# A two-layer encoder step on one core: weight subtractions moved from GpSimd to VectorE in one stage, a sum of squares and bias tiles rearranged in another

## The chip, the core and the metric

The kernel runs on one NeuronCore of a Trainium2 chip. TensorE (PE in the profile) multiplies matrices, VectorE (DVE), ScalarE (ACT) and GpSimd (POOL) work element by element, and SyncE (SP) issues most of the transfers. Each engine takes its own list of instructions strictly in order and waits on semaphores for the others. The metric is device microseconds for one execution: a median of 976.74 us over three runs (975.36 to 978.28).

## The reference

The input is 256 prompt frames and 32 sample frames of width 1024, 288 columns in all, and 256 memory tokens. There are two layers, each with a mixer, a cross-attention into the memory and an MLP. The mixer of layer 0 projects to q, k and v and runs two kinds of softmax attention side by side, 8 heads each: A (a band with a bias by relative position) and B (with a decay made of summed log gates). The mixer of layer 1 is C, stick-breaking attention with 16 heads. Cut to what the change touches:

```python
# memory, both layers: RMS norm over the 1024 features, then k and v
k, v = jnp.split(rmsnorm(mem, g_mem) @ w_kv, 2, axis=-1)
k = rmsnorm(k.reshape(b, n, N_HEADS_X, HEAD_DIM_X), k_gain)

# B: s + decay, masked, softmax;  decay = c_q - c_k
s = jnp.where(ok, s + decay.astype(jnp.float32), NEG)
p = jax.nn.softmax(s, axis=-1)

# C: weights from log_sigmoid(-z), summed from the right
log_keep = jnp.where(before, jax.nn.log_sigmoid(-z), 0.0)
tail = lax.cumsum(log_keep, axis=3, reverse=True) - log_keep
w = jnp.where(before, jnp.exp(jax.nn.log_sigmoid(z) + tail), 0.0)
```

## The kernel before, in words

**Split products.** Activations lie with features on the partitions and the 288 columns along the free axis. Each fp32 operand is split into a high part (`h`, rounded to the PE's reduced fp32 format) and a low part (`l`, the rest), and a product is the three matmuls high·high, high·low, low·high (`mm3`, lines 158 to 160). A weight chunk is 1024 x 256 numbers. `load_chunk` (L118) loads it in two halves into `raw`, one of four buffers shared with the memory's features (`mraw`). ScalarE, or for every n-th piece VectorE (L141), rounds a piece of two rows of blocks into `wh` (L143), and VectorE, or for every n-th piece GpSimd, subtracts it from `raw` into `wl` (L144). The table `STEP` gives each stage the piece's size, which piece's subtraction goes to GpSimd, and which piece's rounding goes to VectorE. A chunk takes 48 matmuls into two PSUM banks out of three (`ps_g`). The next chunk starts in the free bank and needs a bank of the last chunk after three matmuls, so an eviction that is late stops PE there.

**Stages.** A and B with the memory's keys of layer 0, then cross-attention and MLP of layer 0, then C with the memory's keys of layer 1, then cross-attention and MLP of layer 1. Outside C a scheduler orders the instructions of every engine when the kernel is built, by its own estimate of times. In C the order on PE is written out by hand.

**A and B** (`ORD_AB`). Steps `q`, `p` and `a` project q and k, project v, and attend, for one group of four heads. `group_ab` (L923) loads a group's bias tiles: `b1` and `bsmp`, and for B `b0`, on which GpSimd adds the query's sum (L937) and sets the causal mask (L938). There is one buffer of each, so a group's tiles are loaded when the group before has read its own. Step `M` (`mem_split`, L300) splits the memory into `mh` and `ml` and sums its squares, on GpSimd, into `mssum`. The products with `ones` (`ps_ms`, L322 and L325) and the inverse roots `memrs` and `memrt` follow in the same step. `K0` to `K3` are the memory's key projections: their products need only `mh` and `ml`, their eviction `tmk` (L357) needs `memrs`.

**C** (`ORD_C`, `Mix`, L552). `Mix` yields the products of the steps `q`, `k`, `v` (projections for groups 0 to 3), `M` (split of the memory) and `m` (its keys) in pieces of 6 or 12 matmuls. `attend_c` (L641) takes them as filling: it asks for q and k of its group, fills 12 matmuls, computes scores `zz` (prompt, two tiles) and `zs` (sample), starts the softplus chain on ScalarE and VectorE, fills 96 matmuls (`FILL_C[0]`), sums with triangular matmuls (L716, L717), fills 30, multiplies by v for the prompt (L484, result read by `oh` and `ol`, L498 and L499) and at once for the sample (L494), whose result lies in the second half of the tile that `ol` reads. The norm of a key `m` (`xnorm`: `sqx`, `sh`, `sl`, two matmuls `ps_xn`) is put on PE 36 matmuls after the products of that key.

Of the kernel before, what the change touches and what calls it, by code (L numbers as in the profile page):

```python
# [14 lines left out]
P = 128  # L15
# [13 lines left out]
HPE = 0  # L29
HPG = 0  # L30
VT2 = 1
ORD_AB = 'qA0 pA0 F qA1 pA1 aA0 qB0 aA1 qB1 M pB0 pB1 aB0 K2 aB1 K0 K3 K1'.split()
ORD_C = 'q0 k0 v0 q1 M k1 v1 q2 m0 k2 v2 q3 k3 v3 m1 m2 m3'.split()
FILL_C = 96, 30
ORD_X = 's1 s2 s3 s0 v0 v1 S v2 v3'.split()
NWARM = 9
SQP = (0, 1, 2, 3)
# [4 lines left out]
VTB = 2  # L42
WR = 4
WS = 12
STEP = {'ab': (2, 4, 0), 'x0': (4, 5, 7), 'm0': (1, 5, 6), 'c': (2, 2, 4), 'x1': (2, 2, 3), 'm1': (2, 5, 0)}
EPS = 1e-6
NEG = -1e30
EOFF = 160
# [3 lines left out]
def body(ctx: ExitStack, tc: tile.TileContext, i: dict, o: dict):  # L52
# [43 lines left out]
    def bank(pool, name):  # L96
        return pool.tile([P, 512], F32, tag="b", name=name)
# [20 lines left out]
    def load_chunk(ap, w=CW, split=2, before=None):  # L118

        nk = KT // split  # L120
        ws = []
        for s in range(split):
            raw = wraw.tile([P, nk, w], F32, tag="raw", name="raw")
            if before is None:
                nc.sync.dma_start(out=raw, in_=ap[:, s * nk:(s + 1) * nk, :])
            nq = min(nk, NQ) if split > 1 else nk
            step = min(nq, R.step) if before is None else 1
            for k in range(0, nk, step):
                if k % nq == 0:
                    wh = wspl.tile([P, nq, w], F32R, tag="wh", name="wh")  # L130
                    wl = wspl.tile([P, nq, w], F32R, tag="wl", name="wl")
                    ws += [(wh[:, j, :], wl[:, j, :]) for j in range(nq)]
                r, src = slice(k % nq, k % nq + step), raw[:, k:k + step, :]
                if before is not None:
                    nc.sync.dma_start(out=src, in_=ap[:, s * nk + k:s * nk + k + 1, :])
                    before(s * nk + k)
                R.count += 1
                e = nc.gpsimd if R.count % R.pool_every == 0 and before is None else dve
                with ahead(HPS):
                    if R.dve_every and R.count % R.dve_every == 0 and before is None:  # L140
                        dve.tensor_copy(wh[:, r, :], src)  # L141
                    else:
                        act(wh[:, r, :], src, AF.Copy)  # L143
                    e.tensor_tensor(wl[:, r, :], src, wh[:, r, :].bitcast(F32), ALU.subtract)  # L144
        return ws
# [154 lines left out]
    def mem_split(layer):  # L300
        mh = spp.tile([P, KT, T], F32R, tag="sp", name="mh")
        ml = spp.tile([P, KT, T], F32R, tag="sp", name="ml")
        if layer == 0:
            ssum = scr.tile([P, T], F32, tag="ssum", name="mssum", bufs=2)
        for k in range(KT):
            if k % 4 == 0:
                raw = wraw.tile([P, 4, NP_], F32, tag="raw", name="mraw")
                nc.sync.dma_start(out=raw, in_=i["memT"][:, k:k + 4, :])
            m = raw[:, k % 4, :]
            g = gT[:, 3, layer, k:k + 1]  # L310
            act(mh[:, k, 0:NP_], m, AF.Copy, scale=g)
            dve.scalar_tensor_tensor(ml[:, k, 0:NP_], m, g, mh[:, k, 0:NP_].bitcast(F32), ALU.mult, ALU.subtract)
            if layer == 0:
                if k == 0:
                    nc.gpsimd.tensor_tensor(ssum[:, 0:NP_], m, m, ALU.mult)
                else:
                    sq = scr.tile([P, T], F32, tag="f", bufs=FB, name="sqm")
                    nc.gpsimd.tensor_tensor(sq[:, 0:NP_], m, m, ALU.mult)
                    nc.gpsimd.tensor_tensor(ssum[:, 0:NP_], ssum[:, 0:NP_], sq[:, 0:NP_], ALU.add)
        if layer == 0:  # L320
            ps = bank(R.m, "ps_ms")
            mm(ps[:, 0:NP_], ones, ssum[:, 0:NP_], start=True, stop=True)  # L322
            rstd_of(ps[:, 0:NP_], NP_, 1.0 / 1024, memrs)
            for j in range(2):
                mm(ps[:, NP_ + j:NP_ + j + 1], ssum[:, j * P:(j + 1) * P], ones[:, 0:1], start=True, stop=True)  # L325
            rstd_of(ps[:, NP_:NP_ + 2], 2, 1.0 / 1024, memrt)
        return mh, ml

    def sum_parts(ps, sel, sq, n):

# [221 lines left out]
    class Mix:  # L552
# [44 lines left out]
        def run(self, steps):  # L597
            xh, xl, rs = self.x
            for step in steps:
                op, g = step[0], int(step[1:] or 0)  # L600
                if op == "M":
                    mem = mem_split(1)
                elif op == "q":
                    qz = R.ph.tile([P, 2, T], F32, tag="qz", name="qz", bufs=QZB[1])
                    yield from self.products(i["sb_w"][g], xh, xl)
                    for p in range(2):
                        dve.scalar_tensor_tensor(qz[:, p, :], self.ps[p][:, 0:T], 0.125, rs, ALU.mult, ALU.mult)  # L607
                    self.done["q", g] = qz
                elif op == "k":
                    kT = R.ph.tile([P, 2, T], F32, tag="kT", name="kT", bufs=KTB[1])  # L610
                    yield from self.products(i["sb_w"][4 + g], xh, xl)
                    for p in range(2):
                        dve.tensor_tensor(kT[:, p, :], self.ps[p][:, 0:T], rs, ALU.mult)
                    nc.gpsimd.dma_start(out=o["ckT"][:, 2 * g:2 * g + 2, :], in_=kT)
                    self.done["k", g] = kT
                elif op == "v":
                    vT = scr.tile([P, 2, T], F32, tag="t2", name="vT")
                    vt = R.ph.tile([P, 3, CW], F32, tag="vt", name="vt", bufs=VTB)

                    nc.gpsimd.memset(vt[:, 2, :], 0.0)  # L620
                    yield from self.products(i["sb_w"][8 + g], xh, xl)
                    for p in range(2):
                        dve.tensor_tensor(vT[:, p, :], self.ps[p][:, 0:T], rs, ALU.mult)
                    nc.gpsimd.dma_start(out=o["cvT"][:, 2 * g:2 * g + 2, :], in_=vT)

                    def turn(p, vT=vT, vt=vt, g=g):
                        turn_v(vT, vt, p)
                        if p:
                            self.done["v", g] = vt

                    self.later(18, lambda turn=turn: turn(0))
                    self.later(36, lambda turn=turn: turn(1))
                else:
                    yield from self.products(i["w_kv"][1, g], *mem, NP_)
                    t = scr.tile([P, 2, T], F32, tag="t2", name="tmk")
                    for d in range(2):
                        dve.tensor_tensor(t[:, d, 0:NP_], self.ps[d][:, 0:NP_], memrs, ALU.mult)
                    self.later(36, lambda t=t, g=g: self.done.update({("m", g): mem_k_norm(1, g, t)}))
            self.mem = mem

    def attend_c(g, qz, kT, vt, ck, cv, oh, ol, fill):  # L641
# [87 lines left out]
        for p, (zz, w) in enumerate(zip(zzs, wps)):  # L729
            pv_prompt(zz[:, 0, :], p, vt, [(block(w, e, 0), block(w, e, 1)) for e in range(2)])  # L730
            put_prompt(oh, ol, kt0 + p, zz[:, 0, :])
        po = zzs[1][:, 1, :]
        pv_sample(po, cv, vt, [pt[:, 0:P], pt[:, P:2 * P], pt[:, 2 * P:384]], lambda p, par: (2 * p + par) * NS)
        put_sample(oh, ol, kt0, po)
# [186 lines left out]
        return project_v("ab_w", 6 * kind + 4 + g, xh, xl, rs, "ab"[kind] + "vT", g)  # L921

    def group_ab(kind, g, qz, kT, vt):  # L923
        b1 = R.ph.tile([P, 4, NP_], F32, tag="b1", name="b1")
        bsmp = R.ph.tile([P, T], F32, tag="bsmp", name="bsmp")
        if kind == 0:
            nc.sync.dma_start(out=b1, in_=i["biasp"][:, 4 * g:4 * g + 4, :])
            nc.gpsimd.memset(b1[0:64, :, 192:256], NEG)
# [1 line left out]
            nc.sync.dma_start(out=bsmp, in_=i["biass"][g])  # L930
        else:
            nc.sync.dma_start(out=b1, in_=cd[4 * g:4 * g + 4, 0:NP_].unsqueeze(0).to_broadcast([P, 4, NP_]))
            b0 = R.ph.tile([P, 4, P], F32, tag="b0", name="b0")
            for j, d in ((0, b0), (1, b1)):
                n = (j + 1) * P
                cqj = cq[:, j, 4 * g:4 * g + 4].unsqueeze(2).to_broadcast([P, 4, n])
# [15 lines left out]
    for step in ORD_AB:  # L952
        op, at = step[0], step[1:]
        kind, g = ("AB".index(at[0]), int(at[1])) if len(at) == 2 else (0, 0)
        if op == "q":
            qk[at] = project_ab(kind, g)
        elif op == "p":
            vs[at] = values_ab(kind, g)
        elif op == "a":
            group_ab(kind, g, *qk[at], vs[at])  # L960
        elif op == "F":
            forget()
        elif op == "M":
            mh, ml = mem_split(0)
        else:
            R.after = last_mm[0].ins if at == "0" else R.after
            mk0[int(at)] = mem_k(0, int(at), mh, ml)
# [141 lines left out]
```

## Time and profile before

| what | value |
|---|---|
| median of three runs | 976.74 us (975.36 to 978.28) |
| the profiled execution's own time | 978.44 us |
| its span, first to last instruction | 976.1 us |
| PE busy | 952.5 us (98%) |
| DVE busy | 691.8 us (71%) |
| ACT busy | 524.8 us (54%) |
| POOL busy | 266.8 us (27%) |
| mean granted TensorE clock | 0.990 |

The profiled execution took 978.44 us, of which 2.3 us lie outside the span. The page lists busy time for each engine and cuts the span into slices, with the granted TensorE clock beside them. A table of waits says which engine stood idle, at which line, and which instruction of another engine ended the wait. The timeline lists instructions with start and duration, both in microseconds.

### The profile page before, as it was taken

To read this page: it belongs to the slowest core of one execution; us is meant where nothing else is said; L and a number is where in the kernel's file an instruction comes from. 1 tells how busy PE (TensorE), PEld (TensorE's weight loads), DVE (VectorE), ACT (ScalarE), POOL (GpSimd) and SP (SyncE) were. 2 spreads that over 40 slices of the span, in tenths; PEclk is the share of its full clock that TensorE was granted. 3 is DMA by queue.
4 is the path that set the end of the run, shared out by engine and by line. 5 is a ranking of instruction groups with operands and counts; after the bars stand their busy time and mean duration, and the time that the engine had idled before them with its cause. 6 is when DMAs were issued, how large, how long until landed. Compare 5 with 4: busy or idle time off the path is not lost. (4 is left out here: it accounts for less than half of the span.)

```text
span 976.1 us, 19332 instructions
## 1 busy us (share of the span) xinstructions
PE 952.5 (98%) x7284; PEld 920.4 (94%) x7284; DVE 691.8 (71%) x1439; ACT 524.8 (54%) x1212; POOL 266.8 (27%) x275
## 2 busy tenths in 40 slices
PE   8999998999999999999999989899999999999998
PEld 8898787999999999999998889899999999999998
DVE  8778857879777766777677566678987766564643
ACT  5667556656446644444447546555544555453531
POOL 4221363311112211121134233344443211111210
PEclk8999998999999999999999999999999999999999
DMA  8554363654455555545546444365444455455552
GB/s 261 185 174 159 103 223 96 219 184 158 153 168 170 173 162 162 172 155 171 167 159 200 141 143 142 116 231 186 146 148 134 158 171 164 163 164 172 163 171 73
DMA packets 50700, 160.01 MB, mean 164 GB/s; under 512 B 6296, under 2 KB 12968, under 8 KB 50352
## 3 DMA queue, kind: packets, MB, share of 16 engines
q1 hardware_dynamic: 46864, 148.69, 47.6%
q0 software_dynamic: 2592, 8.92, 2.3%
q10 hardware_dynamic: 1152, 1.18, 0.4%
q8 instruction: 57, 0.93, 0.4%
q14 instruction: 35, 0.29, 0.1%
HBM read 148.65 MB, written 10.12 MB: 163 GB/s over the span
## 5 line engine op out<-in xcount | busy, mean ns | idle before, releaser
L143 ACT ACTIVATE wh<-raw 128x512 fp32r<-128x512 f32 (+3 forms) x541 | 269.2, 547 | 234.0 <-PE g L159 107.6
L144 DVE TENSOR_TENSOR wl<-raw,wh 128x512 fp32r<-128x512 f32 (+3 forms) x459 | 309.6, 707 | 99.4 <-ACT wh L143 94.5
L144 POOL TENSOR_TENSOR wl<-raw,wh 128x512 fp32r<-128x512 f32 (+2 forms) x165 | 209.1, 1268 | 532.8 <-ACT wh L143 410.6
L158 PE MATMUL g<-xh,wh 128*128 128x288 f32 (+1 forms) x1032 | 305.0, 299 | 2.9 <-DVE qz L607 1.8
L159 PE MATMUL g<-xl,wh 128*128 128x288 f32 (+1 forms) x1032 | 304.3, 297 | 1.8 <-DVE xl L196 1.8
L160 PE MATMUL g<-xh,wl 128*128 128x288 f32 (+1 forms) x1032 | 303.2, 297 | 0.1
L158 PEld LDWEIGHTS g<-xh,wh 128*128 128x128 f32 (+1 forms) x1032 | 192.9, 188 | 5.0 <-DVE qz L607 2.6
L159 PEld LDWEIGHTS g<-xl,wh 128*128 128x128 f32 (+1 forms) x1032 | 193.5, 188 | 2.7 <-DVE xl L196 2.2
L160 PEld LDWEIGHTS g<-xh,wl 128*128 128x128 f32 (+1 forms) x1032 | 193.1, 188 | 2.6 <-DVE wl L144 1.3
L159 PE MATMUL g<-hl,wh 128*128 128x288 f32 x512 | 150.3, 295 | 0.0
L158 PE MATMUL g<-hh,wh 128*128 128x288 f32 x512 | 149.0, 295 | 0.0
L160 PE MATMUL g<-hh,wl 128*128 128x288 f32 x512 | 148.7, 294 | 0.0
L159 PEld LDWEIGHTS g<-hl,wh 128*128 128x128 f32 x512 | 96.1, 188 | 0.0
L160 PEld LDWEIGHTS g<-hh,wl 128*128 128x128 f32 x512 | 95.8, 188 | 0.0
L158 PEld LDWEIGHTS g<-hh,wh 128*128 128x128 f32 x512 | 95.3, 187 | 0.0
L159 PE MATMUL g<-ol,wh 128*128 128x288 f32 x256 | 75.1, 295 | 0.0
L160 PE MATMUL g<-oh,wl 128*128 128x288 f32 x256 | 74.6, 295 | 0.0
L158 PE MATMUL g<-oh,wh 128*128 128x288 f32 x256 | 74.1, 295 | 0.0
L141 DVE CAST wh<-raw 128x256 fp32r<-128x256 f32 (+2 forms) x83 | 31.9, 384 | 46.3 <-PE g L159 24.5
L867 DVE TENSOR_TENSOR h<-h,g 128x288 f32<-128x288 f32 x64 | 28.8, 450 | 29.7 <-PE g L160 29.6
L159 PEld LDWEIGHTS g<-ol,wh 128*128 128x128 f32 x256 | 48.0, 188 | 0.0
L160 PEld LDWEIGHTS g<-oh,wl 128*128 128x128 f32 x256 | 48.0, 188 | 0.0
(285 smaller groups left out, 1500.0 us busy)
## 6 DMA issues: line engine op xcount, KB each, us to landing
raw<-in_w_up_dram SPq DMA_DIRECT2D x64, 512.0 KB, 3.8
raw<-in_w_down_dram SPq DMA_DIRECT2D x64, 512.0 KB, 3.8
raw<-in_w_kv_dram SPq DMA_DIRECT2D x32, 512.0 KB, 3.9
raw<-in_sb_w_dram SPq DMA_DIRECT2D x24, 512.0 KB, 3.8
raw<-in_ab_w_dram SPq DMA_DIRECT2D x22, 512.0 KB, 5.0
raw<-in_w_q_dram SPq DMA_DIRECT2D x16, 512.0 KB, 4.4
raw<-in_w_o_dram SPq DMA_DIRECT2D x16, 512.0 KB, 4.0
raw<-in_ab_wo_dram SPq DMA_DIRECT2D x8, 512.0 KB, 4.8
```

What stands on the lines that cost most here:

```text
L141: dve.tensor_copy(wh[:, r, :], src)
L143: act(wh[:, r, :], src, AF.Copy)
L144: e.tensor_tensor(wl[:, r, :], src, wh[:, r, :].bitcast(F32), ALU.subtract)
L158: mm(out, lh, rh, start=first, stop=False)
L159: mm(out, lh, rl, start=False, stop=False)
L160: return mm(out, ll, rh, start=False, stop=last)
L867: dve.tensor_tensor(h[:, kt, :], h[:, kt, :], ps[:, 0:T], ALU.add)
```

## The change

In C, `pool_every` becomes 0: all subtractions of weights are VectorE's. A third filling of 12 matmuls stands between the prompt's and the sample's product with v. The order of steps changes: the memory is split after group 1's projections instead of before them, and the keys `m0` and `m1` stand elsewhere. In A and B, `b1`, `bsmp` and `b0` get two buffers each. The memory's squares are ScalarE's and their sums VectorE's. The products with `ones` become a step `N` of their own (`mem_rms`) behind `aB0`, held behind the last projection issued by then.

```diff
-ORD_AB = 'qA0 pA0 F qA1 pA1 aA0 qB0 aA1 qB1 M pB0 pB1 aB0 K2 aB1 K0 K3 K1'.split()
-ORD_C = 'q0 k0 v0 q1 M k1 v1 q2 m0 k2 v2 q3 k3 v3 m1 m2 m3'.split()
-FILL_C = 96, 30
+ORD_AB = 'qA0 pA0 F qA1 pA1 aA0 qB0 aA1 qB1 M pB0 pB1 aB0 N K2 aB1 K0 K3 K1'.split()
+ORD_C = 'q0 k0 v0 q1 k1 v1 M q2 k2 m0 v2 q3 k3 m1 v3 m2 m3'.split()
+FILL_C = 96, 30, 12
-STEP = {..., 'c': (2, 2, 4), ...}
+STEP = {..., 'c': (2, 0, 4), ...}
-                e = nc.gpsimd if R.count % R.pool_every == 0 and before is None else dve
+                e = nc.gpsimd if R.pool_every and R.count % R.pool_every == 0 and before is None else dve
...
-                    nc.gpsimd.tensor_tensor(ssum[:, 0:NP_], m, m, ALU.mult)
+                    act(ssum[:, 0:NP_], m, AF.Square)
...
-                    nc.gpsimd.tensor_tensor(sq[:, 0:NP_], m, m, ALU.mult)
-                    nc.gpsimd.tensor_tensor(ssum[:, 0:NP_], ssum[:, 0:NP_], sq[:, 0:NP_], ALU.add)
-        if layer == 0:
-            ps = bank(R.m, "ps_ms")
...
-        return mh, ml
+                    act(sq[:, 0:NP_], m, AF.Square)
+                    dve.tensor_tensor(ssum[:, 0:NP_], ssum[:, 0:NP_], sq[:, 0:NP_], ALU.add)
+        return mh, ml, ssum if layer == 0 else None
+
+    def mem_rms(ssum):
+        ps = bank(R.m, "ps_ms")
+        mm(ps[:, 0:NP_], ones, ssum[:, 0:NP_], start=True, stop=True)
+        rstd_of(ps[:, 0:NP_], NP_, 1.0 / 1024, memrs)
+        for j in range(2):
+            mm(ps[:, NP_ + j:NP_ + j + 1], ssum[:, j * P:(j + 1) * P], ones[:, 0:1], start=True, stop=True)
+        rstd_of(ps[:, NP_:NP_ + 2], 2, 1.0 / 1024, memrt)
...
             put_prompt(oh, ol, kt0 + p, zz[:, 0, :])
+        fill(FILL_C[2])
         po = zzs[1][:, 1, :]
...
-        b1 = R.ph.tile([P, 4, NP_], F32, tag="b1", name="b1")
-        bsmp = R.ph.tile([P, T], F32, tag="bsmp", name="bsmp")
+        b1 = R.ph.tile([P, 4, NP_], F32, tag="b1", name="b1", bufs=2)
+        bsmp = R.ph.tile([P, T], F32, tag="bsmp", name="bsmp", bufs=2)
...
-            b0 = R.ph.tile([P, 4, P], F32, tag="b0", name="b0")
+            b0 = R.ph.tile([P, 4, P], F32, tag="b0", name="b0", bufs=2)
...
+        elif op == "N":
+
+            with tc.issue_after(last_mm[0].ins):
+                mem_rms(msum)
```

Three places show how the instructions move. Line numbers of the changed kernel are one higher than before from L329 on, and two higher from L733 on.

GpSimd in the second half of A and B. `mssum` and `sqm` are the memory's squares and their sum; `b_2051` and `b_2048` are the bias tiles of the second group of B. Before:

```order
L319 TENSOR_TENSOR mssum<-mssum,sqm 128x256
L519 MEMSET prs 128x96
L319 TENSOR_TENSOR mssum<-mssum,sqm 128x256 x3
L937 TENSOR_TENSOR b_2051<-b_2048,cq 128x512
L319 TENSOR_TENSOR mssum<-mssum,sqm 128x256
L938 AFFINE_SELECT b_2051<-b_2051 128x512
L937 TENSOR_TENSOR b_2048<-b_2048,cq 128x1024
L319 TENSOR_TENSOR mssum<-mssum,sqm 128x256
L938 AFFINE_SELECT b_2048<-b_2048 128x1024
```

And of the change, where these tiles now stand right behind those of the first group of B (`b_1786`, `b_1783`):

```order
L939 TENSOR_TENSOR b_1786<-b_1783,cq 128x512
L940 AFFINE_SELECT b_1786<-b_1786 128x512
L939 TENSOR_TENSOR b_1783<-b_1783,cq 128x1024
L144 TENSOR_TENSOR wl<-raw,wh 128x512
L940 AFFINE_SELECT b_1783<-b_1783 128x1024
L144 TENSOR_TENSOR wl<-raw,wh 128x512
L441 MEMSET vt 128x256
L520 MEMSET prs 128x96
L939 TENSOR_TENSOR b_2051<-b_2048,cq 128x512
L940 AFFINE_SELECT b_2051<-b_2051 128x512
L939 TENSOR_TENSOR b_2048<-b_2048,cq 128x1024
```

The second group's bias moved ahead of the projections of v, and the sum of squares is gone from this engine.

ScalarE in C, at the end of the first group's attention: `oh` is the evicted result (two prompt tiles, then the sample), `mh` the split of the memory. Before:

```order
L725 ACTIVATE wts<-ps_ws 128x384
L143 ACTIVATE wh<-raw 128x512 x2
L498 ACTIVATE oh_6667<-zz 128x256 x2
L503 ACTIVATE oh_6667<-zz 128x2x32
L143 ACTIVATE wh<-raw 128x512
```

Of the change:

```order
L726 ACTIVATE wts<-ps_ws 128x384
L143 ACTIVATE wh<-raw 128x512 x2
L499 ACTIVATE oh_6667<-zz 128x256
L311 ACTIVATE mh<-mraw,gT 128x256 x6
L499 ACTIVATE oh_6667<-zz 128x256
L311 ACTIVATE mh<-mraw,gT 128x256 x2
L143 ACTIVATE wh<-raw 128x512
L504 ACTIVATE oh_6667<-zz 128x2x32
```

Six splits of the memory came between the two prompt tiles.

VectorE in C, in the last group's softplus chain. `sp`, `spl`, `sps` and the scan into `zsb` (printed under the name SCALAR_TENSOR_TENSOR) are of that chain; `tmk`, `sqx`, `sh` and `sl` are of the norm of a memory key. Before, that key's rows came behind the chain:

```order
L707 SCALAR_TENSOR_TENSOR zsb<-sps 128x288
L708 TENSOR_TENSOR ws<-zsb 128x288
L637 TENSOR_TENSOR tmk<-g,memrs 128x256 x2
L144 TENSOR_TENSOR wl<-raw,wh 128x512
L344 TENSOR_TENSOR sqx<-sqx 128x256
L332 CAST sh<-sqx 128x256
L141 CAST wh<-raw 128x512
L334 TENSOR_TENSOR sl<-sqx,sh 128x256
```

Of the change:

```order
L638 TENSOR_TENSOR tmk<-g,memrs 128x256 x2
L700 SCALAR_TENSOR_TENSOR sp<-zz,a 128x768
L705 TENSOR_TENSOR spl<-sp,sph 128x768
L144 TENSOR_TENSOR wl<-raw,wh 128x512 x2
L345 TENSOR_TENSOR sqx<-sqx 128x256
L141 CAST wh<-raw 128x512
L700 SCALAR_TENSOR_TENSOR sps<-zsb 128x288
L333 CAST sh<-sqx 128x256
L705 TENSOR_TENSOR spl<-sp,sph 128x768
L144 TENSOR_TENSOR wl<-raw,wh 128x512 x2
L708 SCALAR_TENSOR_TENSOR zsb<-sps 128x288
L335 TENSOR_TENSOR sl<-sqx,sh 128x256
```

The key's evictions moved into the chain, ahead of most of it, and its last step `sl` now stands behind the scan that ends it. On PE the two `ps_xn` matmuls that read `sh` and `sl` stand 36 matmuls behind the key's last product.

More of the change, by code (lines that the diff above doesn't have):

```diff
@@ L44 @@
 WS = 12
-STEP = {'ab': (2, 4, 0), 'x0': (4, 5, 7), 'm0': (1, 5, 6), 'c': (2, 2, 4), 'x1': (2, 2, 3), 'm1': (2, 5, 0)}
+STEP = {'ab': (2, 4, 0), 'x0': (4, 5, 7), 'm0': (1, 5, 6), 'c': (2, 0, 4), 'x1': (2, 2, 3), 'm1': (2, 5, 0)}
 EPS = 1e-6
@@ L314, in mem_split @@
                 if k == 0:
-                    nc.gpsimd.tensor_tensor(ssum[:, 0:NP_], m, m, ALU.mult)
+                    act(ssum[:, 0:NP_], m, AF.Square)
                 else:
                     sq = scr.tile([P, T], F32, tag="f", bufs=FB, name="sqm")
-                    nc.gpsimd.tensor_tensor(sq[:, 0:NP_], m, m, ALU.mult)
-                    nc.gpsimd.tensor_tensor(ssum[:, 0:NP_], ssum[:, 0:NP_], sq[:, 0:NP_], ALU.add)
-        if layer == 0:
-            ps = bank(R.m, "ps_ms")
[L322 to L326, printed above, removed]
-        return mh, ml
+                    act(sq[:, 0:NP_], m, AF.Square)
[8 more added lines that the diff above has]
+        rstd_of(ps[:, NP_:NP_ + 2], 2, 1.0 / 1024, memrt)
     def sum_parts(ps, sel, sq, n):
@@ L601, in run @@
                 if op == "M":
-                    mem = mem_split(1)
+                    mem = mem_split(1)[0:2]
                 elif op == "q":
@@ L963, in body @@
         elif op == "M":
-            mh, ml = mem_split(0)
+            mh, ml, msum = mem_split(0)
+        elif op == "N":
+            with tc.issue_after(last_mm[0].ins):
+                mem_rms(msum)
         else:
```

## The prediction

> **What bounds the kernel now.** I read the stretches of the span first, then PE's waits. In the two rows the columns are the stretch, then busy us (and count) of PE, PE's weight loads, DVE, ACT and POOL, then the granted clock, the DMA share and GB/s.
>
> ```profile
> 165.00:500.00 335.00, 335.00 (x2576) 330.94 (x2575) 250.57 (x547) 177.85 (x440) 71.84 (x76) 1.00 0.53 170
> 500.00:650.00 150.00, 140.94 (x1164) 132.58 (x1163) 100.13 (x151) 85.44 (x171) 51.70 (x47) 1.00 0.48 157
> ```
>
> From 165 to 500 us PE never stops: 2576 matmuls in 335 us, 0.13 us each. There nothing but fewer matmuls would help, and the change takes none away. C (500 to 650 us) has 9.1 us in which PE is idle. PE's list of waits (total us, times, longest) says where:
>
> ```profile
> PE zz L494 <- DVE ol L499: 3.9, 4, 1.6
> PE g L158 <- DVE qz L607: 2.8, 3, 1.0
> PE ps_ms L322 <- POOL mssum L319: 2.4, 1, 2.4
> PE s L527 <- DVE mx L468: 2.3, 2, 1.9
> PE g L158 <- DVE tmk L637: 1.6, 1, 1.6
> PE g L158 <- DVE kT L613: 0.7, 1, 0.7
> PE pos L494 <- ACT pts L546: 0.6, 1, 0.6
> PE ps_pt L533 <- ACT pt L537: 0.6, 1, 0.6
> PE ps_ms L325 <- ACT memrs L182: 0.6, 1, 0.6
> ```
>
> Rows 1, 2, 5 and 6 are C's, 9.0 us. The other five are 6.5 us in A and B. The second price is the clock:
>
> ```profile
> 107.40:110.80 3.40, 3.40 (x15) 2.22 (x14) 3.13 (x13) 1.30 (x4) 0.00 (x0) 0.50 0.70 195
> 144.90:148.30 3.40, 1.35 (x27) 1.00 (x27) 0.65 (x2) 1.10 (x3) 3.40 (x4) 1.00 0.31 122
> 148.40:155.20 6.80, 5.38 (x17) 4.30 (x18) 4.05 (x23) 3.96 (x15) 1.82 (x3) 0.50 0.00 0
> 570.00:577.00 7.00, 5.39 (x65) 4.66 (x64) 4.31 (x9) 2.76 (x7) 1.58 (x2) 1.00 0.34 112
> ```
>
> After the stops of 1.9 and 2.4 us in A and B the granted clock is 0.50 for 3.4 and 6.8 us; C's 1.6 us stop (in the last row) leaves it at 1.00. So a stop of about 2 us costs a second time.
>
> **C: the subtractions.** GpSimd's 33 subtractions go to VectorE. What they cost now is seen in the first group's chain (start, duration, engine):
>
> ```profile
> 524.48 0.95 DVE L704 TENSOR_TENSOR spl<-sp,sph 128x768 fp32r<-128x768 f32 x1
> 525.34 0.69 DVE L144 TENSOR_TENSOR wl<-raw,wh 128x512 fp32r<-128x512 f32 x1
> 526.01 1.98 DVE L704 TENSOR_TENSOR spl<-sp,sph 128x768 fp32r<-128x768 f32 x1
> 528.62 1.77 DVE L144 TENSOR_TENSOR wl<-raw,wh 128x512 fp32r<-128x512 f32 x1
> 525.45 1.72 POOL L144 TENSOR_TENSOR wl<-raw,wh 128x512 fp32r<-128x512 f32 x1
> 528.46 1.38 POOL L144 TENSOR_TENSOR wl<-raw,wh 128x512 fp32r<-128x512 f32 x1 [1.29 <-issue]
> 530.76 0.29 PE L160 MATMUL g<-xh,wl 128*128 128x288 f32 x1
> 531.97 0.40 PE L158 MATMUL g<-xh,wh 128*128 128x288 f32 x1 [0.92 <-DVE qz L607]
> L144 POOL TENSOR_TENSOR wl<-raw,wh 128x512 fp32r<-128x512 f32 x33 | 46.6, 1411 | 53.0 <-PE g L160 23.2 <-ACT wh L143 22.8 <-issue 5.3
> L144 DVE TENSOR_TENSOR wl<-raw,wh 128x512 fp32r<-128x512 f32 x32 | 35.8, 1120 | 4.0 <-ACT wh L143 4.0
> ```
>
> A VectorE subtraction takes 0.69 us alone and 1.77 beside GpSimd's, `spl` 0.95 and 1.98: about 1.05 us is lost wherever the two meet. VectorE's own 32 have a mean of 1.12, so 0.43 x 32 = 13.8 us is lost on them, and some 8 us more on `spl` and others; the 33 taken over cost 33 x 0.69 = 22.8. VectorE's load hardly changes (100 of 150 us); what changes is where it stands. So the sum goes by places.
>
> First group, boundary q1 to k1 (the 0.92 above): two meetings saved, -1.03 and -1.08, two subtractions taken over, +1.38, and `qz` now stands ahead of `ws` (0.46): about 1.2 us earlier. The wait of 0.92 goes. So does the 0.7 on `kT`: the memory's split that stood between the two evictions moves away.
>
> Second group: PE comes to the boundary q2 to k2 after 60 filling matmuls where it was 72, so 12 x 0.13 = 1.6 us sooner; VectorE loses its two meetings and gets `vT` earlier, 1.4 to 1.9 us. A wait of 0.6 to 1.2 stays for the 0.95 before; I take 0.8. Third group: q3's boundary goes behind the triangular sums, but the one of v2, 51 matmuls into the filling, comes before `vT`, which now stands behind both `spl` and `sps`; 0.9 stays.
>
> **C: the sample's values later.** 12 or 18 matmuls now stand ahead of L494, 1.6 to 2.3 us, over waits of up to 1.6; groups 2 to 4 lose theirs. Not the first:
>
> ```profile
> 542.45 0.38 ACT L498 ACTIVATE oh<-zz 128x256 fp32r<-128x256 f32 x1 [0.44 <-PE zz L484]
> 543.10 0.38 ACT L498 ACTIVATE oh<-zz 128x256 fp32r<-128x256 f32 x1 [0.27 <-PE zz L484]
> 512.39 1.71 ACT L311 ACTIVATE mh<-mraw,gT 128x256 fp32r<-128x256 f32 x4 [2.25 <-DMA mraw<-in_memT_dram]
> L499 DVE TENSOR_TENSOR ol<-zz,oh 128x256 fp32r<-128x256 f32 x8 | 3.3, 418 | 1.8 <-ACT oh L498 1.8
> ```
>
> ScalarE has six `mh` between the two `oh`: four take 1.71, so six 2.45. The second `ol` then ends 0.35 + 2.45 + 0.38 + 0.42 = 3.6 us behind the first `oh`'s start, with hand-overs 3.75. PE ends the second prompt tile 0.65 behind it (542.45, 543.10) and its 18 matmuls 2.35 later, at 3.0: it waits 0.75. The row of 3.9 becomes 0.75.
>
> **C: the wait that takes the place.** The key m1 ends early in the last group's filling, and PE meets its `ps_xn` 36 matmuls later, 36 x 0.13 = 4.7 us. VectorE's queue to `sl` is in-order: the second `tmk`, `sp`, `spl`, two `wl`, `sqx`, a rounding, `sps`, `sh`, `spl`, two `wl`, the scan, `sl`.
>
> ```profile
> 641.96 0.41 DVE L344 TENSOR_TENSOR sqx<-sqx 128x256 f32<-128x256 f32 x1
> L699 DVE SCALAR_TENSOR_TENSOR sp<-zz,a 128x768 f32<-128x768 f32 x8 | 7.6, 953 | 2.1 <-ACT a L698 2.1
> L637 DVE TENSOR_TENSOR tmk<-g,memrs 128x256 f32<-128x256 f32 x8 | 3.3, 421 | 5.0 <-PE g L160 4.9
> L707 DVE TENSOR_TENSOR_SCAN zsb<-sps 128x288 f32<-128x288 f32 x4 | 3.0, 745 | 0.0
> L334 DVE TENSOR_TENSOR sl<-sqx,sh 128x256 fp32r<-128x256 f32 x3 | 1.3, 418 | 0.0
> L332 DVE CAST sh<-sqx 128x256 fp32r<-128x256 f32 x3 | 0.8, 282 | 0.0
> ```
>
> 0.42 + 0.95 + 0.95 + 1.38 + 0.41 + 0.41 + 0.45 + 0.28 + 0.95 + 1.38 + 0.74 + 0.42 = 8.7 us (the rounding and `sps` as the rows near them), less 13 overlaps of some 0.08 (525.34 begins 0.09 before the 0.95 from 524.48 is over): 7.7. PE stands 7.8 - 4.7 = 3.1 us at the second `ps_xn`; everything of PE's is behind it. It takes the place of the 1.6 on `tmk`. Bounds: nothing, if `sl` were done first, and 3.5. I take 3.1, as each of its terms has a row. A stop that long is over the 1.9 us that halved the clock, so 3.4 us at 0.50, 1.7 us.
>
> The Trainium skill (TensorE: Matmul & The Clock Gate, "What's actually happening") has the clock fall only after at least one idle window of about 3.4 us. By that 3.1 us would cost nothing more and the total came out 1.7 us lower; here stops of 1.9 us were followed by half the clock, so the trace disagrees and decides.
>
> Sum for C: waits 9.0 to 0.75 + 0.8 + 0.9 + 3.1 = 5.55, so -3.45. Each stop also costs a restart (530.76 to 531.97 is 1.21, of it 0.92 wait and 0.13 the matmul: 0.16); five fewer, -0.8. Clock +1.7. **C: -2.6 us.**
>
> **A and B.** GpSimd stands behind both remaining trouble spots:
>
> ```profile
> 100.71 2.09 POOL L937 TENSOR_TENSOR b<-b,cq 128x1024 f32<-128x1024 f32 x1
> 100.97 2.14 DVE L334 TENSOR_TENSOR sl<-sqh,sh 128x288 fp32r<-128x288 f32 x1
> 103.37 2.83 DVE L144 TENSOR_TENSOR wl<-raw,wh 128x512 fp32r<-128x512 f32 x1
> 148.48 0.72 POOL L319 TENSOR_TENSOR mssum<-mssum,sqm 128x256 f32<-128x256 f32 x1
> 125.00:150.00 25.00, 20.94 (x169) 17.62 (x168) 12.13 (x26) 11.00 (x28) 19.02 (x23) 0.97 0.56 185
> ```
>
> The last partial sum stood behind the second B group's bias and ended at 149.2, when PE had nothing else. With sums on VectorE and both bias tiles early, PE has key products and softmax left to mix. In its order the first `ps_ms` comes after 60 of the memory's 256-column products, the other products of that chunk follow, and only then those that need `tmk`. So the waits on `mssum`, `memrs`, `pts`, `pt` and the small part (0.4) of the `mx` row go: 2.4 + 0.6 + 0.6 + 0.6 + 0.4 = 4.6. The eight squares and seven sums (3.2 us on ScalarE by `mh`'s 0.43, 2.9 on VectorE by `tmk`'s 0.42) lie under PE's products: VectorE is busy 12.1 of 25 us there. If that cover is gone they cost 2.9.
>
> The halved 6.8 us behind it go; 0.9 and 0.6 us of them were waits, so half of 5.3, -2.7. The 1.9 us stop, from VectorE held by the first B bias (2.14 for an `sl` of 0.42, 2.83 for a 0.69), stays with its half clock: the bias is added by the same GpSimd instructions. The second bias now runs among projections too; bounds 0 (hidden) and 2 us (as the first), I take 0.6, as there is more filling. New is the end: PE's order mixes so many of the output projection's products in early that at the last group only L494 is left, and what needs it. A wait as on `pts` (0.6) and one as C's on `ol` (0.7) come back: +1.3. Restarts: two fewer, -0.3. **A and B: -4.6 - 2.7 + 0.6 + 1.3 - 0.3 = -5.7 us.**
>
> **Sum.** 978.44 - 2.6 - 5.7 = 970.1 for an execution like the profiled one, which lies 1.7 above the median of 976.74: **968.4 us**.
>
> **Rivals.** (1) All of C's waits go but the first group's: then `sl` is in time, the clock stays, and C gives -9.0 + 0.75 - 1.3 = -9.5, in all 961.5. For it: 1.05 us is freed at every meeting. Against it: the queue to `sl` above, which holds no meeting at all.
>
> (2) A and B give nothing: the second bias among projections holds VectorE as the first did, 1.9 + 1.7 for the clock, and at the end the two waits halve the clock once more, 1.7; 0.6 of it was counted. -5.7 + 4.7 = -1.0, and in all 973 to 974, hardly to be told from no change. For it: 2.83 us for a 0.69 subtraction. Against it: GpSimd's sums in between are gone.
>
> (3) Slower: VectorE's queue becomes C's bound. Every chunk then has two more subtractions ahead of the eviction that frees a bank. If the meetings saved do not lie ahead of the same evictions, each of the 12 boundaries inside the groups pays 2 x 0.69 = 1.4, 16.8 us for the 5.1 of evictions now, with the stop at `ps_xn` and its clock 16.8 - 5.1 + 3.1 + 1.7 = +16.5; with 3.1 won at L494 and 5.7 in A and B, less the 1.7 to the median, in all about 984. It decides when VectorE is busy beyond some nine tenths of C; it is at 100 of 150 us. The Trainium skill (Perfetto Trace Analysis, "Optimizing Scalar/DVE Operations") holds that with VectorE saturated, moving work to ScalarE or even GpSimd may make sense, which speaks against this change; the same sentence's neighbour adds that the two share a port, so it might not help, and here VectorE isn't saturated.
>
> **How the numbers follow.** Forecast 0.46 (965 to 972), rival 1 0.21 (958 to 965), rival 2 0.18, rival 3 0.13, the rest between. The range takes in the first three and reaches a little beyond no change: 958 to 979. What can be told from no change is some 0.3%, 2.9 us: faster 0.70, same 0.16, slower 0.14.
>
> **What would show it.** Right: no GpSimd subtraction between 500 and 650 us and VectorE's all near 0.69; L494 (now L495) waits once, in the first group; a stop of 2.5 to 3.5 us at `ps_xn` in the last group with a clock of 0.50 behind it; `ps_ms` without a wait; two short stops before the output projection of A and B. Wrong: `ps_xn` without a wait (rival 1), a second stop of 2 us between 105 and 130 us (rival 2), waits at every chunk boundary in C (rival 3).

## The result: faster by 0.6%, where 0.9% was forecast

The changed kernel takes 972.34 us (median of 5 runs, 969.47 to 972.9) against 976.74 us (975.3 to 978.28): a ratio of 0.9938, 95% interval 0.9914 to 0.9961. Ratios, here and below, are estimated from the fast executions alone and are not the quotients of the medians beside them (here 0.9955). So the gain is 4.4 us by the medians and 6.1 by the ratio, which is also what lies between the two profiled executions. The forecast was 968.4 us, in a range of 958 to 979. The profiled execution took 972.34 us, with a span of 970.6.

PE's waits in the changed kernel (total us, times, longest), without the rows of the stages that the change leaves alone:

```profile
PE ps_xn L337 <- DVE sl L335: 2.6, 1, 2.6
PE g L158 <- DVE qz L608: 2.0, 1, 2.0
PE ps_pt L534 <- ACT pt L538: 1.8, 1, 1.8
PE zz L495 <- DVE ol L500: 1.1, 1, 1.1
PE s L528 <- DVE mx L469: 1.1, 2, 0.7
PE g L158 <- DVE vT L624: 0.9, 1, 0.9
PE pos L495 <- ACT pts L547: 0.6, 1, 0.6
```

L494's 3.9 us are down to 1.1, and the waits on `mssum`, `memrs` and `tmk` are gone. Three stops are new: `ps_xn` (forecast), `qz` in one piece of 2.0 us where three of up to 1.0 stood, and `ps_pt` with 1.8 where it had 0.6.

How the time divides is read from a matmul that stands at a fixed place of the work, `ps_rs`, the sum for a norm: of the fourteen, the seventh stands at the start of the MLP of layer 0 and the eleventh at that of the cross-attention of layer 1, behind C. Before, and then the changed kernel (start, duration):

```profile
300.26 0.41 PE L215 MATMUL ps_rs<-ssum,ones 128*128 128x288 f32 x1
679.17 0.41 PE L215 MATMUL ps_rs<-ssum,ones 128*128 128x288 f32 x1
```

```profile
295.25 0.41 PE L215 MATMUL ps_rs<-ssum,ones 128*128 128x288 f32 x1
673.84 0.41 PE L215 MATMUL ps_rs<-ssum,ones 128*128 128x288 f32 x1
```

A and B give 5.0 us (forecast 5.7); the stretch with C goes from 378.9 to 378.6, 0.3 us (forecast 2.6). The rest of the span and what lies outside it (2.3 before, 1.7 now) give 0.8 together.

Stretches of the changed kernel (us; then busy us and count of PE, weight loads, DVE, ACT, POOL; granted clock, DMA share, GB/s):

```profile
93.16:96.56 3.40, 2.06 (x31) 1.45 (x29) 3.40 (x10) 3.40 (x11) 1.96 (x2) 1.00 0.21 61
96.57:99.98 3.41, 2.67 (x10) 2.27 (x11) 3.38 (x13) 1.52 (x4) 0.18 (x1) 0.50 0.57 185
99.99:103.39 3.40, 3.40 (x16) 3.40 (x15) 1.31 (x6) 0.99 (x4) 0.00 (x0) 0.50 0.76 246
500.00:650.00 150.00, 143.14 (x1167) 134.63 (x1167) 97.35 (x188) 87.27 (x176) 7.15 (x16) 0.99 0.49 158
622.22:625.60 3.38, 3.38 (x17) 3.38 (x16) 2.58 (x6) 2.33 (x5) 1.08 (x2) 0.50 0.33 116
```

VectorE has taken 33 subtractions over in C and is busy 97 us instead of 100; two groups of its operations show why:

```profile
L144 DVE TENSOR_TENSOR wl<-raw,wh 128x512 fp32r<-128x512 f32 x64 | 41.5, 687 | 4.9 <-ACT wh L143 3.5
L705 DVE TENSOR_TENSOR spl<-sp,sph 128x768 fp32r<-128x768 f32 x8 | 7.6, 951 | 0.0
```

Each of the 64 takes 0.69 us, where 32 took 1.12, and `spl` 0.95 where it took 1.33.

### The profile page after: what moved, and what is told of

It is laid out like the page before. It is cut to its first block, busy times and chain, and to the rows that moved or that the text cites. A ratio compares the mean times of both kernels' runs of the same rounds, so it can differ in the third digit from the quotient of the medians.

```text
span 970.6 us, 19260 instructions
## 1 busy us (share of the span) xinstructions
PE 950.4 (98%) x7284; PEld 919.9 (95%) x7284; DVE 684.5 (71%) x1486; ACT 525.7 (54%) x1220; POOL 198.6 (20%) x220
## 4 chain that ended last, share of the span: by engine, by line
PE 90%; DVE 4%; ACT 2%; issue 2%; DMA 1%; POOL 0%; SPq 0%; DVEq 0%; POOLq 0%
PE g L158 27%; PE g L160 26%; PE g L159 26%; DVE wl L144 1%; PE zz L717 1%; PE po L485 1%; PE s L528 1%; PE zz L485 1%; PE zz L672 0%; DMA raw<-in_ab_w_dram 0%; PE sx L160 0%; PE sx L158 0%; PE pox L160 0%; PE ps_px L786 0%; PE sx L159 0%
## 5 line engine op out<-in xcount | busy, mean ns | idle before, releaser
L144 POOL TENSOR_TENSOR wl<-raw,wh 128x512 fp32r<-128x512 f32 (+3 forms) x125 | 152.9, 1223 | 478.5 <-ACT wh L143 363.9
L158 PEld LDWEIGHTS g<-oh,wh 128*128 128x128 f32 x256 | 47.5, 188 | 0.4 <-ACT oh L504 0.4
```

The source lines that it names most:

```text
L158: mm(out, lh, rh, start=first, stop=False)
```

## The experiments

All ratios are to the kernel before on the same chip; the changed kernel's own is 0.9938, measured on the first one. Diffs are against the changed kernel unless said otherwise.

### Which half of the change gives the time

A and B alone:

```diff
-ORD_C = 'q0 k0 v0 q1 k1 v1 M q2 k2 m0 v2 q3 k3 m1 v3 m2 m3'.split()
-FILL_C = 96, 30, 12
+ORD_C = 'q0 k0 v0 q1 M k1 v1 q2 m0 k2 v2 q3 k3 v3 m1 m2 m3'.split()
+FILL_C = 96, 30, 0
-... 'c': (2, 0, 4) ...
+... 'c': (2, 2, 4) ...
```

> Only the A and B half of the change; C keeps its order, its two fillings and GpSimd's 33 subtractions. Theory P (the time adds up by places, nearly all of the gain is A and B's): the span lies 5.0 us under that of the kernel before, the median near 971.7, and C's 9 us of waits stand as before. Rival S (half of the gain is C's subtractions, as the fall of the waits from 9.1 to 6.9 us after 300 us suggests): about 974.5.

C alone, made from the kernel before:

```diff
-ORD_C = 'q0 k0 v0 q1 M k1 v1 q2 m0 k2 v2 q3 k3 v3 m1 m2 m3'.split()
-FILL_C = 96, 30
+ORD_C = 'q0 k0 v0 q1 k1 v1 M q2 k2 m0 v2 q3 k3 m1 v3 m2 m3'.split()
+FILL_C = 96, 30, 12
-... 'c': (2, 2, 4) ...
+... 'c': (2, 0, 4) ...
+        fill(FILL_C[2])
         po = zzs[1][:, 1, :]
```

> Only C's half of the change; A and B as before. Theory P: C gains 0.3 us, so 976.4, with a stop of 2.0 us on qz at C's start, one of 2.6 us at the second ps_xn of the last group and 3.4 us of half clock behind that. Rival S: half of the measured gain, about 974.5. Rival T (the two new stops of C come only with the shift that A and B bring): without them, 971.5.

Measured: A and B alone 972.65 us against 978.34, ratio 0.9945 (0.9926 to 0.9963); C alone 976.92, ratio 0.9991 (0.9976 to 1.0007). The product is 0.9936, the changed kernel's 0.9938: the halves add up, and C's cannot be told from nothing. In C's own run the new stops stand as in the whole change:

```profile
PE ps_xn L336 <- DVE sl L334: 2.6, 1, 2.6
PE g L158 <- DVE qz L607: 2.0, 1, 2.0
```

Its `ps_rs` stand at 300.90 and 679.47, 378.6 us apart, 0.3 less than before. With A and B alone they stand at 294.91 and 675.20, 380.3 us apart: the waits of C are those of before, and a window of half clock has come into it. Theory P holds; S and T fall.

### C's pieces: subtractions and third filling

Every second subtraction back on GpSimd:

```diff
-... 'c': (2, 0, 4) ...
+... 'c': (2, 2, 4) ...
```

> The whole change, but every second subtraction of C is GpSimd's again, as before. Theory P (the subtractions move 2 to 3 us by places and cost 2.0 at C's start, so nothing net): the stop at C's start is gone, waits of 0.9 us on qz or kT come back at two or three chunk ends, ratio 0.993 to 0.995. Rival S (GpSimd's subtractions are what C loses by, 14 us of VectorE's time): ratio 0.997 or more.

Measured: 973.32 us, ratio 0.9938 (0.9914 to 0.9962), the changed kernel's to the fourth place. The longest of its waits in C:

```profile
PE g L158 <- DVE qz L608: 1.9, 2, 1.0
PE ps_xn L336 <- DVE sh L333: 1.6, 1, 1.6
PE ps_xn L337 <- DVE sl L335: 1.4, 1, 1.4
```

The 2.0 us stop at C's start is gone; two waits of about 1 us on `qz` are back, and the last group's stop comes in two parts. Theory P holds: the subtractions by themselves are worth nothing that the ratios show. In this one execution C's stretch, from 294.81 to 674.47, is 1.1 us longer than the changed kernel's.

No third filling:

```diff
-FILL_C = 96, 30, 12
+FILL_C = 96, 30, 0
```

> The whole change without the third filling: the sample's values follow the prompt's at once, the 12 matmuls go to the end. Theory P (a wait at L495 is PE's own time): L495 waits again 0.9 to 1.6 us in groups 2 to 4, about 2.7 us more in all, ratio 0.9965. Rival X (the time gained at L495 was lost again at the next boundary, since the same VectorE queue follows): no difference, 0.994.

Measured: 979.93 us, ratio 1.0016 (0.9996 to 1.0036), over twice the loss that theory P gave, and X gave none.

```profile
PE ps_xn L337 <- DVE sl L335: 5.2, 2, 2.6
PE zz L495 <- DVE ol L500: 5.0, 3, 3.1
```

L495 costs 5.0 instead of 1.1, of it 3.1 in the first group: there the six `mh` between the two `oh` are uncovered, as the prediction's chain had it (3.75 us behind the first `oh`, less the 0.65 by which PE's second tile ends later). The rest was in neither theory: 12 matmuls fewer ahead of each group move the end of the key m0 into the third group's filling. There its `sl` stands behind the scan (584.75 us, the scan at 584.09), a second stop of 2.6. So the filling is what makes C's half of the change no loss. C's order of steps was not run by itself.

### C's start

PE's `ps_rs` and its stop, the two rows of ScalarE that `qz` needs with what stands between them, and (last two rows) VectorE, in the changed kernel:

```profile
499.94 0.65 PE L215 MATMUL ps_rs<-ssum,ones 128*128 128x288 f32 x2
503.39 0.40 PE L158 MATMUL g<-xh,wh 128*128 128x288 f32 x1 [2.01 <-DVE qz L608]
500.63 0.50 ACT L182 ACTIVATE rs<-ps_rs,epsb 128x288 f32<-128x288 f32 x1 [2.73 <-PE ps_rs L215]
501.02 1.14 ACT L143 ACTIVATE wh<-raw 128x512 fp32r<-128x512 f32 x2
502.07 0.43 ACT L183 ACTIVATE rs<-rs 128x288 f32<-128x288 f32 x1
501.68 1.29 DVE L144 TENSOR_TENSOR wl<-raw,wh 128x512 fp32r<-128x512 f32 x2 [2.64 <-ACT wh L143]
502.89 0.82 DVE L608 SCALAR_TENSOR_TENSOR qz<-g,rs 128x288 f32<-128x288 f32 x2
```

Before, the halves of `rs` followed each other:

```profile
504.29 0.65 PE L215 MATMUL ps_rs<-ssum,ones 128*128 128x288 f32 x2
504.98 0.50 ACT L182 ACTIVATE rs<-ps_rs,epsb 128x288 f32<-128x288 f32 x1 [2.07 <-PE ps_rs L215]
505.51 0.44 ACT L183 ACTIVATE rs<-rs 128x288 f32<-128x288 f32 x1
```

Three lists have changed. PE has six matmuls between `ps_rs` and the stop where it had eleven, so `ps_rs` comes 5 x 0.13 = 0.7 us later. ScalarE has two roundings between the halves: the second starts 1.44 us behind the first where it started 0.53 behind, 0.9 more. VectorE has two subtractions ahead of `qz`, which starts 0.39 us behind the end of `rs` where it started 0.04 behind, 0.35 more. With the 0.1 us that PE stood there before, that is the stop of 2.0. With GpSimd on every second piece of the first two chunks alone, the order of before is back in all three lists:

```diff
-... 'c': (2, 0, 4) ...
+... 'c': (2, 2, 4) ...
                     self.done["k", g] = kT
+                    R.pool_every = 0
```

> The whole change, but every second subtraction of C's first two chunks stays on GpSimd; by the order ScalarE then no longer puts two roundings between the two halves of rs, and PE gets ps_rs five matmuls earlier. Theory V (the 2.0 us stop on qz at C's start comes from this order, 1.2 us of roundings plus two subtractions ahead of qz): the stop falls to 0.1, the time by 2.0 to 970.2. Rival W (the stop comes of the VectorE time that the subtractions take there, and GpSimd's return brings the meetings back): 971.5 to 972.5, with a wait of 1 us on qz or kT in the first chunks.

Measured: 968.70 us (965.99 to 971.82), ratio 0.9912 (0.9882 to 0.9942). The row on `qz` is gone from its waits, no wait on `kT` came, and the stretch from 292.75 to 669.43 is 1.9 us shorter than the changed kernel's. By places V holds; the interval of the ratio alone would not show it, as it touches the changed kernel's. The run puts all three lists back at once, so what each is worth is read from the rows above and not from a run.

### The stop at ps_xn

VectorE's last rows up to `sl`, and PE's second `ps_xn`, in the changed kernel:

```profile
618.21 0.95 DVE L705 TENSOR_TENSOR spl<-sp,sph 128x768 fp32r<-128x768 f32 x1
619.07 1.29 DVE L144 TENSOR_TENSOR wl<-raw,wh 128x512 fp32r<-128x512 f32 x2
620.28 0.75 DVE L708 TENSOR_TENSOR_SCAN zsb<-sps 128x288 f32<-128x288 f32 x1
620.95 0.40 DVE L335 TENSOR_TENSOR sl<-sqx,sh 128x256 fp32r<-128x256 f32 x1
621.40 0.39 PE L337 MATMUL ps_xn<-sl,onesr 128*128 128x256 f32 x1 [2.61 <-DVE sl L335]
```

VectorE is not idle in these rows; PE, whose first `ps_xn` starts at 618.44, is ahead of its queue. First, `sl` on the idle GpSimd:

```diff
-        (nc.gpsimd if HNP else dve).tensor_tensor(sl[:, 0:n], ...
+        (nc.gpsimd if R.c else dve).tensor_tensor(sl[:, 0:n], ...
```

> The whole change, but in C the subtraction sl of a norm runs on GpSimd, which has nothing else there, and so no longer stands behind VectorE's softplus chain. Theory Q (the 2.6 us stop at ps_xn is VectorE's queue and halves the clock behind it): the stop shrinks to about 0.6 us, the clock stays at 1.00, 2.0 + 1.7 = 3.7 us less than the changed kernel's 972.3: 968.6. Rival U (PE then meets v3's eviction vT, which stands in the same queue, and stops there): the stop moves on, 0.5 to 1.5 us less, 971 to 972.

Measured: 972.69 us, ratio 0.9943 (0.9920 to 0.9965), no gain. Neither theory was right: the stop stayed where it was, at 2.8, since GpSimd's `sl` took 3.17 us, beside four operations of VectorE back to back. Beside one short operation of VectorE the same `sl` took 0.73 us, at 577.67 and 637.49 us of that run.

```profile
618.79 3.17 POOL L335 TENSOR_TENSOR sl<-sqx,sh 128x256 fp32r<-128x256 f32 x1 [13.66 <-DVE sh L333]
618.62 0.95 DVE L705 TENSOR_TENSOR spl<-sp,sph 128x768 fp32r<-128x768 f32 x1
619.49 1.29 DVE L144 TENSOR_TENSOR wl<-raw,wh 128x512 fp32r<-128x512 f32 x2
620.69 0.75 DVE L708 TENSOR_TENSOR_SCAN zsb<-sps 128x288 f32<-128x288 f32 x1
```

Then more of PE's work put over the queue, by order alone. The 60 holds for every key of C, the 24 for the last group:

```diff
-                    self.later(36, lambda t=t, g=g: ...mem_k_norm(1, g, t)
+                    self.later(60, lambda t=t, g=g: ...mem_k_norm(1, g, t)
-        fill(FILL_C[0])
+        fill(FILL_C[0] - 24 * (g == 3))
...
+        fill(24 * (g == 3))
         pp = bank(ps_t, "ps_ws")
```

> The whole change, but in C's last group 72 instead of 96 matmuls fill before the triangular sums (the 24 come right behind them), and a memory key's norm stands 60 instead of 36 matmuls behind its key; the work is the same. Theory Q (the stop of 2.6 us at ps_xn is PE standing 3 us ahead of VectorE's queue and halves the clock behind it): the triangular sums, 3 us of PE that need only spl, cover the queue, the stop and the 3.4 us at 0.50 go, 2.6 + 1.7 = 4.3 less than the changed kernel, a ratio of 0.990 to before. Rival U (the queue only shows up at the next thing that PE needs of it, vT or ws): a stop of 1 to 2 us there, ratio 0.992 to 0.994.

Measured: 969.00 us (966.45 to 969.65), ratio 0.9896 (0.9866 to 0.9925), 4.1 us less than the changed kernel by the ratios, whose intervals overlap a little. By places C's stretch, from 294.69 to 670.89, is 2.4 us shorter, although a window of half clock, worth 1.7, has come to C's start. The row on `ps_xn` is gone; what shows up next is small, as U had it in kind and not in size:

```profile
PE g L158 <- DVE vT L624: 0.7, 1, 0.7
PE ps_ws L725 <- ACT vt L434: 0.7, 1, 0.7
```

There is no half clock behind the place any more. Theory Q holds.

### A and B: the second buffers, and GpSimd beside the softmax

One buffer each:

```diff
-        b1 = R.ph.tile([P, 4, NP_], F32, tag="b1", name="b1", bufs=2)
+        b1 = R.ph.tile([P, 4, NP_], F32, tag="b1", name="b1")
```

and the same for `bsmp` and `b0`.

> The whole change, but b1, bsmp and b0 of A and B have one buffer each, as before. Theory B (the second buffer is what lets GpSimd add B's bias 18 us earlier, under other work): the stop of 1.9 us on mx near 104 us is back, the second group's bias runs where VectorE has the memory's sums; about half of the 5 us of A and B is lost, ratio 0.9965. Rival N (A and B gain by the squares and the sum behind the projections alone): no difference to the changed kernel, 0.994.

Measured: 970.05 us (967.57 to 972.04), ratio 0.9915 (0.9886 to 0.9944). Theory B falls: nothing is lost. N holds as far as the ratios go. The stop of 1.9 us on `mx` is not back, and no `ps_pt` is among its longest waits from 80 to 200 us. The first of them, and the one on `mx`:

```profile
PE pos L495 <- ACT pts L547: 0.7, 1, 0.7
PE s L528 <- DVE mx L469: 0.4, 1, 0.4
```

Its `ps_rs` ahead of the MLP of layer 0, from the timeline:

```profile
291.62 0.41 PE L215 MATMUL ps_rs<-ssum,ones 128*128 128x288 f32 x1
```

By this execution A and B gain 8.6 us without the second buffers. With them and the same order in A and B, nine kernels of this study reach that matmul at 292.75 to 295.66, a gain of 4.6 to 7.5. Whether the buffers cost time is not settled by the ratios, whose intervals overlap; no run shows that they win any. The squares and the step `N`, which then make the gain, were not run apart.

What they bring instead is seen at 94 us, where in the changed kernel GpSimd has nothing but a weight subtraction to do and does it beside VectorE's scaling of `pr`. The timeline (start, duration), and then the four scalings as a group (least, middle and longest in ns):

```profile
94.24 1.70 POOL L144 TENSOR_TENSOR wl<-raw,wh 128x512 fp32r<-128x512 f32 x1 [9.76 <-ACT wh L143]
96.99 0.47 PE L534 MATMUL ps_pt<-ident,pr 128*128 128x128 f32 x1 [1.76 <-ACT pt L538]
```

```profile
L476 DVE TENSOR_SCALAR pr<-pr,ri x4: 269/318/1627, 94.7 to 96.9; 128x256 f32<-128x256 f32 x2, 128x128 f32<-128x128 f32 x2
```

One scaling of 1.63 us stands among ones of 0.3. In all nine executions with this A and B such a scaling (1.61 to 1.63) and this stop (1.55 to 1.77) are there; with one buffer each no scaling of that stage is so slow. No GpSimd subtraction in A and B:

```diff
-STEP = {'ab': (2, 4, 0), ...
+STEP = {'ab': (2, 0, 0), ...
```

> The whole change, and in A and B too all subtractions of weights are VectorE's (17 were GpSimd's). Theory Y (the 1.8 us stop at ps_pt at 95 us, followed by half clock to 103.4, comes from the GpSimd subtraction of 1.70 us beside which VectorE's scaling of pr took 1.63 instead of 0.35): the stop falls to 0.5, at least one window of half clock goes, 3 us less than the changed kernel, ratio 0.991. Rival Z (VectorE is busy 132 of 165 us there, 17 x 0.69 = 12 us more put evictions late): new waits of PE on VectorE in A and B, ratio 0.994 to 0.998.

Measured: 972.60 us, ratio 0.9925 (0.9895 to 0.9955). The stop at `ps_pt` fell from 1.8 to 0.4, no scaling there is slow, and no half clock followed it, as Y said. But waits that were not there came, as Z said:

```profile
PE g L158 <- DVE vT L447: 1.1, 1, 1.1
PE po L485 <- DVE ol L505: 1.0, 1, 1.0
```

The cause of the stop is shown; whether the edit is worth making stays open.

### Putting it together

Both mends of C:

```diff
-... 'c': (2, 0, 4) ...
+... 'c': (2, 2, 4) ...
+                    R.pool_every = 0
-                    self.later(36, ...
+                    self.later(60, ...
-        fill(FILL_C[0])
+        fill(FILL_C[0] - 24 * (g == 3))
+        fill(24 * (g == 3))
```

> Both mends of C in one: every second subtraction of the first two chunks on GpSimd, and in the last group the triangular sums 24 matmuls sooner with the key's norm 60 matmuls behind. Theory (stops of different places add up): 2.0 + 0.2 at C's start and 4.1 in the last group less than the changed kernel's 0.9938, about 0.9875. Rival (the windows of half clock fall elsewhere and give 2 to 3 us back): 0.990.

Measured: 966.17 us (965.20 to 967.04), ratio 0.9879 (0.9860 to 0.9899). From 294.76 to 667.54 C's stretch is 372.8 us, 5.8 less than in the changed kernel: the two stops and their clock add up. This version is faster than both kernels, its interval lying below the changed kernel's.

Two more edits on it. The split of the memory behind k2:

```diff
-... k1 v1 M q2 k2 m0 v2 ...
+... k1 v1 q2 k2 M m0 v2 ...
```

> As the run with both mends, and the split of the memory stands behind k2 instead of v1, so that no mh stands between the two oh of the first group. Theory (the 1.1 us stop at L495 is ScalarE's six mh): the stop goes, 1.1 us less, 0.9865. Rival (the split now is late for m0 and PE waits for ml or mh there): a new wait of 1 to 3 us at m0's start, 0.988 to 0.990.

and, with that, no GpSimd subtraction in A and B:

```diff
-STEP = {'ab': (2, 4, 0), ...
+STEP = {'ab': (2, 0, 0), ...
```

> As the run before it, with all subtractions of A and B on VectorE as well. Theory Y (the stop at ps_pt with its half clock goes): 1.3 us and, where the window falls so, 1.7 more: 0.985. Rival Z (the new waits on vT and ol that the run with this edit alone showed cost as much): no difference.

Measured: 967.63 us, ratio 0.9895 (0.9873 to 0.9916), and 967.78, ratio 0.9899 (0.9878 to 0.9921): no gain from either. In the first the 1.1 us at L495 are gone, and more has come back, not at m0 but on v (of these rows about 0.7 and 0.2 were there):

```profile
PE g L158 <- DVE vT L625: 1.5, 2, 0.8
PE ps_vt L431 <- ACT vt L434: 1.1, 1, 1.1
```

In the second the stop at `ps_pt` is down to 0.4, but PE waits 1.8 us on a `vT` of A and B and 2.3 on one of C, as rival Z had it in kind. The two mends of C with one buffer each in A and B were not run together.

## Why the prediction was right, and where it was off

The direction and the range were right, the size was not: 4.4 us won by the medians for 8.3 forecast. The 3.9 us between are 2.3 in C, 0.7 in A and B, 1.7 from the last step, less the 0.8 behind C and outside the span. That the total stayed well inside the range is in part luck, since C gave almost nothing and A and B came near by errors that for the most part cancel.

**C, -2.6 forecast, -0.3 measured.** From 500 to 650 us PE is idle 9.06 us before and 6.86 in the changed kernel, so 2.2 were won where the sum had 3.45. The clock gave 1.7 back, as forecast. The 0.8 for five fewer restarts did not come: C's stretch without PE's idle time and without half of its time at 0.50 is 369.9 us before and 370.0 now, and 369.1 to 370.3 in all fourteen executions, whether PE idles 2.9 us in it or 12.2. That leaves 0.2 of the 2.3 missing.

Of the waits, those in the sum came near. L495 waits once, in the first group, 1.1 us for 0.75: between the second `oh` and its `ol` VectorE has a rounding and an `ml` (540.32 to 541.05 us), which the sum left out. The boundary after q1 and the wait on `kT` went; v2's `vT` waits 0.9 for 0.9; the second group's 0.8 did not come. `ps_xn` stands 2.6 for 3.1 (the prediction's terms gave 7.7 us of queue, and it went on with 7.8), with one window of half clock behind it. These are 0.95 us better than forecast in sum. The term that failed was left out: C's start. "So the sum goes by places" went from the boundary q1 to k1 onward and took q0's `qz`, 0.1 us before, as unmoved; there the stop is 2.0 us. Its cause is no meeting of engines but the order of three engines' lists, which could have been read ahead of the run.

**A and B, -5.7 forecast, -5.0 measured,** near by errors that for the most part cancel; the nine executions with this A and B gave 4.6 to 7.5. The waits on `mssum`, `memrs` and `pt` and the halved 6.8 us behind them went as forecast, and 0.9 us of stops before the output projection answer to 1.3. But "The 1.9 us stop ... stays with its half clock" failed: the row on `mx` holds 1.1 us in two pieces. The first B bias, added at 100.7 us before, is added at 79.9 now; but the stop need not come with it, since with one buffer each it is added at 102.2 and the row on `mx` is 0.4. What took the stop away stays open. And the 1.8 us at `ps_pt`, with two windows at 0.50, were not in the sum. Rival 2 had the mechanism, GpSimd holding VectorE in the softmax, at another place and through a weight subtraction; the sum of the rival, next to nothing from A and B, fell.

**The median, -1.7 forecast.** The execution profiled before lay 1.7 us above its kernel's median, the one of the changed kernel on it. What one profile differs from its median by need not be shared by the next one; one window of half clock more or less, below, is enough to make it.

**The rivals.** Rival 1 fell with the 2.6 us at `ps_xn`. Rival 3 fell: no wait at every chunk's boundary, and VectorE busy 97 of 150 us. The Trainium skill's sentence on moving work off VectorE (Perfetto Trace Analysis, "Optimizing Scalar/DVE Operations") had its caveat borne out: at that place `sl` on GpSimd took 3.17 us where VectorE took 0.40.

## What to carry to other kernels

Moving work off a shared resource pays at the place where a wait ends last and nowhere else: 33 subtractions moved for nothing that the ratios show, while 24 matmuls put in another order were worth some 4 us. When a change alters what a scheduler sees, read each engine's new order at every place where the critical engine restarts, also where the profile shows no wait now. A stop is priced with the clock behind it, and a single execution can carry a window or two of half clock more than another of the same code, so compare stretches of several.

## What the runs showed of the hardware

**The half clock goes by windows that stand on a grid.** In each execution the edges of all stretches at 0.50 lie a whole number of 3.41 us apart (changed kernel: 7.8, 96.6, 622.2; 26 and 180 windows from the first). So it matters how a stop lies on the grid. The same stop of 2.0 us at C's start, in the changed kernel and in the run with the earlier triangular sums:

```profile
499.35:502.76 3.41, 2.03 (x14) 1.69 (x12) 1.08 (x2) 1.87 (x4) 0.00 (x0) 1.00 0.49 156
502.77:506.18 3.41, 2.79 (x21) 2.79 (x22) 0.94 (x3) 0.59 (x2) 0.00 (x0) 1.00 0.47 149
```

```profile
500.69:504.10 3.41, 1.40 (x11) 1.26 (x10) 2.03 (x4) 1.84 (x5) 0.00 (x0) 1.00 0.32 109
504.11:507.50 3.39, 3.39 (x16) 3.39 (x15) 0.43 (x1) 0.44 (x1) 0.00 (x0) 0.50 0.33 117
```

In the first, 1.38 us of it fall into one window and the rest into the next, and the clock stays; in the second one window holds all of it, and the next runs at 0.50. Worked out from PE's records in eight executions on their grids: all 13 windows at full clock with 1.87 us idle or more were followed by half clock, none of those with under 1.2, and of 16 between 1.25 and 1.82 nine. The other six executions add five windows of 2.01 us or more, all followed by half clock, and none under 1.2 that was. So that "C's 1.6 us stop ... leaves it at 1.00" was chance: with A and B alone changed, a window of C with 1.60 us idle was followed by half clock, where the kernel before had 1.61. The Trainium skill (TensorE: Matmul & The Clock Gate, "What's actually happening") has these free-running windows of 3413 ns, and the trace agrees; by its table the clock falls after an idle window, and here windows idle for a little over half of their length were always enough.

**VectorE's operations on a single large input lose to GpSimd too, and GpSimd loses as well.** Beside a GpSimd addition of 1.89 us a rounding `sh` of 0.31 us took 2.03, and beside a subtraction of 1.70 a scaling of 0.35 took 1.63; each reads one large tile. The other way round, GpSimd's `sl` took 3.17 us beside four VectorE operations, each of its usual length, and 0.73 elsewhere. The Trainium skill (SBUF — State Buffer, "SBUF: two separate sides") has the two engines share a pair of ports under an exclusive lock, held for a whole instruction; that agrees with operations that are late by the length of the other's, while the four in a row are more than one instruction.
